# Entry of a ConvFFN's down projection: eight low halves by ScalarE and adding DMAs instead of VectorE and GpSimd

## The chip, the core and the metric

The kernel runs on one core of a Trainium2 chip. A core has TensorE (PE, the matmuls), VectorE (DVE), ScalarE (ACT), GpSimd (POOL) and SyncE (SP), each with an instruction queue of its own that is worked through in order, and 16 DMA engines that the queues of SP, ACT and POOL feed. The metric is the device time of one execution in microseconds (us), lower is better.

## The reference, cut to what matters

The program is one decoder layer: a gated linear attention and a conformer convolution side by side, merged, and then a gated ConvFFN. What the change touches is the last line of the ConvFFN:

```python
u = rms_norm(h, norm_ffn_g[l])
a, bv = jnp.split(u @ w_up[l], 2, axis=-1)
a = causal_dwconv(a, ffn_dw_w[l], ffn_dw_b[l])
h = h + (jax.nn.silu(a) * bv) @ w_down[l]
...
h = rms_norm(h, final_norm_g)
```

The inner width is 2816 (22 tiles of 128 channels), the model width 1024 (8 tiles), and there are 1024 tokens. All is float32.

## The kernel before

**Three matmuls for one.** Every float32 operand x of a matmul is split in two: hi is x rounded to float32r (ACT copies x with AF.Copy into a float32r tile), lo is x - hi, rounded likewise. `mm3` (L178 to L189) gives each product of a weight tile and an operand tile as three matmuls: hi with hi (L187), the weight's hi with the operand's lo (L188), the weight's lo with the operand's hi (L189). In the tiles' names wr is a raw weight piece, wh and wl its halves; ar is a raw activation pair, oph and opl its halves.

**How lo is made.** In the ordinary way DVE (or POOL) subtracts: `lo = raw - hi` (L162 for weights, L228 for operands). `load_w` with POOL as its engine has another way, which the first 51 weight pieces of the program take: ACT writes hi, and also writes the negated rounded value into lo (scale -1, L173); then a DMA issued by POOL adds the raw weight from HBM onto lo (L175, `accum_op=ALU.add`), so that no engine subtracts.

**The stage around the change.** The up projection ends with unit 21 (`unit_head`, `unit_products`: eight products of 24 matmuls; `unit_tail`: taps, Silu, product with the gate, on DVE and ACT). Each unit's result is written to HBM (act_d). The down projection takes the tokens in two halves of 512 (hf 0 and 1). For a half, `load_act` loads the activations of one pair of channel tiles (ar, 128 x 1024) by a DMA issued on POOL (L898) and splits it; there are ten such pairs and an eleventh that is split from SBUF, from the results of units 20 and 21. The weight of an output tile comes in three pieces (8, 8 and 6 channel tiles wide); output tiles 0 and 1 are worked together, so the pieces come as tile 0 first piece (here w0), tile 1 first piece (w1), tile 0 second piece (w2), then w3, w4, w5. One piece of 8 channel tiles against four pairs is 24 matmuls of 512 columns. w0 and w1 need the pairs 0 to 3, w2 and w3 the pairs 4 to 7, w4 and w5 the pairs 8 to 10.

**What sets the order.** A tile scheduler places the instructions; in this stretch `rate["pinned"]` is on, and every ACT copy that makes a hi half is kept in the program's order. The program calls `load_act` for the pairs in turn, with the loads of w0, w1 and w2 behind the pairs 1, 5 and 9. Within a queue an instruction that waits holds back all that stand behind it, a DMA's issue on POOL too. Raw weights have three buffers, hi and lo three each; the activations, their halves and the residual tiles share 35 slots.

Of the kernel before, what the change touches and what calls it, by code (L numbers as in the profile page):

```python
# [11 lines left out]
F32R = mybir.dt.float32r  # L12
U8 = mybir.dt.uint8
AF = mybir.ActivationFunctionType
ALU = mybir.AluOpType
# [24 lines left out]
HT = 516  # L40
# [24 lines left out]
def build(ctx, tc, xT, w_mix, w_o3, w_up, w_dn, w_au, pvec, masks, outT):  # L65
    nc = tc.nc
    V, S, PO, PE = nc.vector, nc.scalar, nc.gpsimd, nc.tensor
# [20 lines left out]
    def slot(dt=F32, nm="s"):  # L88
        uid[0] += 1
        return slots.tile([P, SLOT], dt, tag="slot", name=f"{nm}_{uid[0]}")  # L90
# [6 lines left out]
    def psum():  # L97
        return bank("prod")[:, :512] if "prod" in banks else bank("mm")
# [37 lines left out]
    def load_alpha(src):  # L136
        with tc.high_priority(offset=10000):
            raw = wraw.tile([P, 1024], F32, tag="raw", name="wr_a")
            hl = wspl.tile([P, 1024], F32R, tag="hi", name="wh_a")
            nc.sync.dma_start(raw, src)  # L140
            S.activation(hl, raw, AF.Copy)
            lo, full = (t.rearrange("p (k n) -> p k n", n=P)[:, :, 96:112] for t in (hl, raw))
            V.tensor_tensor(lo, full, lo.bitcast(F32), op=ALU.subtract)
        return hl, None

    def pin(ins):
        if rate["pinned"]:
            tc.keep_in_program_order(ins)

    def load_raw(src):  # L150
        uid[0] += 1
        raw = wraw.tile([P, 1024], F32, tag="raw", name=f"wr_{uid[0]}")[:, : src.shape[-1]]
        nc.sync.dma_start(raw, src)
        return raw

    def split_w(raw, eng=None):
        uid[0] += 1
        n = raw.shape[-1]
        hi = wspl.tile([P, 1024], F32R, tag="hi", name=f"wh_{uid[0]}")[:, :n]
        lo = wspl.tile([P, 1024], F32R, tag="lo", name=f"wl_{uid[0]}")[:, :n]  # L160
        pin(S.activation(hi, raw, AF.Copy))  # L161
        (eng or V).tensor_tensor(lo, raw, hi.bitcast(F32), op=ALU.subtract)  # L162
        return hi, lo

    def load_w(src, eng=None, ahead=4000):
        with tc.high_priority(offset=ahead):
            raw = load_raw(src)
            if eng is not PO:
                return split_w(raw, eng)
            uid[0] += 1  # L170
            hi = wspl.tile([P, 1024], F32R, tag="hi", name=f"wh_{uid[0]}")
            lo = wspl.tile([P, 1024], F32R, tag="lo", name=f"wl_{uid[0]}")
            pin(S.activation(lo, raw, AF.Copy, scale=-1.0))  # L173
            pin(S.activation(hi, raw, AF.Copy))
            nc.gpsimd.dma_start(lo, src, accum_op=ALU.add)  # L175
            return hi, lo

    def mm3(out, whi, wlo, pairs, cols, first=True, last=True):  # L178
        n = len(pairs)
        c0, c1 = cols  # L180
        if wlo is None:
            for k, (wk, (hi, lo)) in enumerate(pairs):
                PE.matmul(out, whi[:, wk], hi[:, c0:c1], start=k == 0, stop=False)
                PE.matmul(out, whi[:, wk], lo[:, c0:c1], start=False, stop=k == n - 1)
            return
        for k, (wk, (hi, lo)) in enumerate(pairs):
            PE.matmul(out, whi[:, wk], hi[:, c0:c1], start=first and k == 0, stop=False)  # L187
            PE.matmul(out, whi[:, wk], lo[:, c0:c1], start=False, stop=False)  # L188
            PE.matmul(out, wlo[:, wk], hi[:, c0:c1], start=False, stop=last and k == n - 1)  # L189

    def operand(t, n=2 * HT, eng=None):
        hi, lo = slot(F32R, "oph"), slot(F32R, "opl")
        split(t[:, :n], hi[:, :n], lo[:, :n], eng)
        return hi, lo

    def block(w, act, chunks, off, evac, mid=None):
        whi, wlo = w
        if mid:
            pts = [psum()[:, :n] for _, n in chunks]
            for k in range(KT):  # L200
                for (c0, n), pt in zip(chunks, pts):
                    mm3(pt, whi, wlo, [(slice(k * P, (k + 1) * P), act[k])], (off + c0, off + c0 + n), k == 0, k == KT - 1)
            rate["pinned"] = True
            mid()
            for (c0, n), pt in zip(chunks, pts):
                pin(evac(pt, c0, n))
            rate["pinned"] = False
            return
        pairs = [(slice(k * P, (k + 1) * P), act[k]) for k in range(KT)]
        for c0, n in chunks:  # L210
            pt = psum()
            mm3(pt[:, :n], whi, wlo, pairs, (off + c0, off + c0 + n))
            evac(pt[:, :n], c0, n)
            tick()
# [11 lines left out]
    def split(src, hi, lo, eng=None):  # L226
        pin(S.activation(hi, src, AF.Copy))
        (eng or V).tensor_tensor(lo, src, hi.bitcast(F32), op=ALU.subtract)  # L228
# [11 lines left out]
        return [tmp512()[:, :n] for i in range(2)] + [None]  # L240

    conv_q, gla_q, ln_q = deque(), deque(), deque()
    rate = {"conv": 0.0, "gla": 0.0, "ln": 0.0, "conv_due": 0.0, "gla_due": 0.0, "ln_due": 0.0, "ahead": 10000, "pinned": False}

    def step(q):
        while q:
# [4 lines left out]
    def tick():  # L251
        for name, q in (("gla", gla_q), ("conv", conv_q), ("ln", ln_q)):
            rate[name + "_due"] = min(rate[name + "_due"] + rate[name], 64.0) if q else 0.0
            while rate[name + "_due"] >= 1.0 and q:
                step(q)
                rate[name + "_due"] -= 1.0
# [34 lines left out]
    order = [NB_A]  # L291
# [8 lines left out]
    w_alpha = seq[0]  # L300
    seq += [w_o3[i] for i in range(16)]
    seq += [w_o3[16 + i] for _ in range(2) for i in range(8)]
    wq = deque()
    wpos = [0]

    def prefetch(n):
        while wpos[0] < len(seq) and len(wq) < n:
            src = seq[wpos[0]]
            wq.append(load_alpha(src) if src is w_alpha else load_w(src, PO if wpos[0] < 51 else V, rate["ahead"]))
            wpos[0] += 1  # L310

    def next_w(ahead=1):
        prefetch(ahead + 1)
        return wq.popleft()
# [65 lines left out]
    def c_pair(i):  # L380
        sg = slot(nm="sg")
        c = slot(nm="c")
        PO.memset(c[:, 0:META], 0.0)
        block(next_w(), u, CHUNKS_L, 0,
              lambda pt, c0, n: S.activation(sg[:, c0 : c0 + n], pt, AF.Sigmoid))
        block(next_w(), u, CHUNKS_L, 0,
              lambda pt, c0, n: V.tensor_tensor(c[:, META + c0 : META + c0 + n], pt, sg[:, c0 : c0 + n], op=ALU.mult))
        conv_q.append(conv(i, c))
# [200 lines left out]
    def r_block(i):  # L589
        og = ogs.pop(i)  # L590
        sr = slot(nm="sr")

        def ev(pt, c0, n):
            sl = slice(c0, c0 + n)
            S.activation(sr[:, sl], pt, AF.Silu)
            PO.tensor_tensor(og[:, sl], og[:, sl], sr[:, sl], op=ALU.mult)

        block(next_w(), u, CHUNKS_Q, T0, ev)
        nc.sync.dma_start(og_d[i], og[:, :LQ])
# [295 lines left out]
    def load_act(hf, j):  # L895
        raw = slot(nm="ar")
        src = act_d[j].rearrange("p (e t) -> p e t", t=SEQ)[:, :, hf * 512 : (hf + 1) * 512]
        nc.gpsimd.dma_start(raw[:, :1024].rearrange("p (e t) -> p e t", t=512), src)  # L898
        return operand(raw, 1024, PO if hf == 0 and j in (8, 9) else V)

    on_pool = (1, 4)
    pieces = [(0, 8), (8, 16), (16, FT)]
# [1 line left out]
    seq[:] = [w_dn[n][:, a * P : b * P] for _ in range(2) for ns in groups for a, b in pieces for n in ns]  # L904
    wpos[0] = len(order)
    seq[:0] = [None] * len(order)

    def finish(hf, c0, cn, h2, pt):
        rs = tmp512()[:, :cn]
        rsqrt_from(pt, rs, cn, RMS_EPS, chunk_tmps(cn))  # L910
        yield 1
        for m in range(KT):
            h = h2[m // 2][:, (m % 2) * 512 + c0 : (m % 2) * 512 + c0 + cn]
            if m in on_pool:
                PO.tensor_tensor(h, h, rs, op=ALU.mult)
            else:
                V.scalar_tensor_tensor(h, h, pcol("fin_g", m), rs, op0=ALU.mult, op1=ALU.mult)
            if m % 2:
                t0 = hf * 512 + c0
                src = h2[m // 2][:, :1024].rearrange("p (e t) -> p e t", t=512)[:, :, c0 : c0 + cn]  # L920
                (nc.sync if m % 4 == 1 else nc.scalar).dma_start(
                    outT[m - 1 : m + 1, :, t0 : t0 + cn].rearrange("e p t -> p e t"), src)
            yield 1
# [3 lines left out]
    for j in range(FT // 2):  # L927
        if j == FT // 2 - 1:
            hi, lo = slot(F32R, "oph"), slot(F32R, "opl")
# [11 lines left out]
    for hf in range(2):  # L941
        if hf:
            acts = [load_act(hf, j) for j in range(FT // 2)]
# [102 lines left out]
```

## Time and profile before

| what | value |
|---|---|
| time, median of 3 runs | 1846.56 us (1845.87 to 1848.41) |
| profiled execution, its own time | 1847.21 us |
| its span, first to last instruction | 1845.4 us |
| PE busy | 1776.2 us (96%) |
| DVE busy | 1156.4 us (63%) |
| ACT busy | 705.6 us (38%) |
| POOL busy | 444.8 us (24%) |
| mean granted TensorE clock | 0.983 |

A time in the rows is counted from the span's first instruction. The matmuls of the down projection begin 1570.88 us into the span. PE's busy time is modelled, and matmuls overlap in it; what PE loses is better read from the starts of its matmuls. In a waits view a line names who waited and for whom, and an idle time in brackets belongs to the instruction behind it. The granted clock is 1.00 at the upper of TensorE's two levels (2.4 GHz) and 0.50 at the lower (1.2 GHz).

### The profile page before, as it was taken

The page shows a single profiled execution, that of the slowest core. Times are in us where ns is not written, and L with a number is a line of the kernel's source. Part 1 is how long each engine was busy: PE and PEld are TensorE (multiplying, and loading weights), DVE is VectorE, ACT ScalarE, POOL GpSimd, SP SyncE. Part 2 cuts the span into 40 slices and gives each one's busy share as a digit, 9 for nine tenths or more (in the row PEclk, how much of TensorE's full clock was granted, in tenths as well). Part 3 has the DMA queues.
Part 4 walks back from the last instruction along what each step waited for, and adds up shares of the span by engine and source line. Part 5 has one row for each costly group of instructions (what it writes and reads, how often), then busy time and mean ns, then how long its engine had stood idle before and what let it go on. Part 6 is the DMA issues. An engine that isn't in the chain of part 4 may idle for free.

```text
span 1845.4 us, 28931 instructions
## 1 busy us (share of the span) xinstructions
PE 1776.2 (96%) x12210; PEld 1692.7 (92%) x12210; DVE 1156.4 (63%) x1350; ACT 705.6 (38%) x1050; POOL 444.8 (24%) x333
## 2 busy tenths in 40 slices
PE   4999999999999999999999997999999999899997
PEld 3999999999999999999999997999999999677886
DVE  5239976968878860733455369877667666733523
ACT  5325436426435743691222333222222223423321
POOL 2103223313413412200000256333333334200000
PEclk7999999999999999999999998999999999999999
DMA  6343335324334544453133441222221224634532
GB/s 211 79 92 87 65 80 125 70 71 114 69 80 103 121 124 120 153 192 137 35 137 129 164 132 35 100 73 77 86 79 69 87 86 151 207 116 154 158 119 66
DMA packets 63442, 200.93 MB, mean 109 GB/s; under 512 B 6864, under 2 KB 14160, under 8 KB 63312
## 3 DMA queue, kind: packets, MB, share of 16 engines
q1 hardware_dynamic: 51168, 159.03, 26.4%
q0 software_dynamic: 10368, 37.75, 10.2%
q10 hardware_dynamic: 1776, 2.30, 0.4%
q8 instruction: 96, 1.57, 0.4%
q14 instruction: 34, 0.28, 0.0%
HBM read 162.31 MB, written 36.74 MB: 108 GB/s over the span
## 4 chain that ended last, share of the span: by engine, by line
PE 80%; DVE 13%; DMA 2%; issue 2%; ACT 2%; POOL 1%; SPq 0%; DVEq 0%; ACTq 0%; POOLq 0%
PE mm L187 13%; PE mm L188 13%; PE mm L189 13%; PE prod L187 12%; PE prod L189 12%; PE prod L188 12%; DVE y L370 5%; DVE opl L228 1%; DVE wl L162 1%; PE g L476 1%; DVE E L445 1%; DMA x<-in_xT 1%; PE g L544 1%; PE g L537 1%; PE g L545 1%
## 5 line engine op out<-in xcount | busy, mean ns | idle before, releaser
L187 PE MATMUL mm<-uh,wh 128*128 128x342 f32 (+4 forms) x1344 | 445.7, 332 | 0.0
L188 PE MATMUL mm<-ul,wh 128*128 128x342 f32 (+4 forms) x1344 | 435.0, 324 | 0.0
L189 PE MATMUL mm<-uh,wl 128*128 128x342 f32 (+4 forms) x1344 | 433.0, 322 | 0.0
L188 PE MATMUL prod<-opl,wh 128*128 128x258 f32 x1232 | 349.7, 284 | 12.1 <-DVE opl L228 11.8
L187 PE MATMUL prod<-oph,wh 128*128 128x258 f32 x1232 | 350.1, 284 | 4.8 <-DVE t L832 4.8
L189 PE MATMUL prod<-oph,wl 128*128 128x258 f32 x1232 | 350.4, 284 | 0.0
L370 DVE SCALAR_TENSOR_TENSOR y<-c,pv,y 128x1026 f32<-128x1026 f32 x240 | 342.3, 1426 | 5.4
L161 ACT ACTIVATE wh<-wr 128x1024 fp32r<-128x1024 f32 (+2 forms) x152 | 147.7, 974 | 382.5 <-PE prod L188 175.2
L162 DVE TENSOR_TENSOR wl<-wr,wh 128x1024 fp32r<-128x1024 f32 (+2 forms) x134 | 159.0, 1189 | 175.6 <-ACT wh L161 174.3
L187 PEld LDWEIGHTS mm<-uh,wh 128*128 128x128 f32 x1344 | 255.7, 190 | 5.4 <-issue 3.7
L188 PEld LDWEIGHTS mm<-ul,wh 128*128 128x128 f32 x1344 | 255.5, 190 | 1.7 <-issue 0.6
L189 PEld LDWEIGHTS mm<-uh,wl 128*128 128x128 f32 x1344 | 255.6, 190 | 0.7 <-issue 0.6
L188 PEld LDWEIGHTS prod<-opl,wh 128*128 128x128 f32 x1232 | 234.4, 190 | 13.3 <-DVE opl L228 12.7
L187 PEld LDWEIGHTS prod<-oph,wh 128*128 128x128 f32 x1232 | 234.4, 190 | 5.8 <-issue 3.2
L189 PEld LDWEIGHTS prod<-oph,wl 128*128 128x128 f32 x1232 | 233.9, 190 | 0.0
L189 PE MATMUL mm<-oph,wl 128*128 128x512 f32 (+1 forms) x374 | 143.6, 384 | 3.2 <-DVE wl L162 3.2
L187 PE MATMUL mm<-oph,wh 128*128 128x512 f32 (+1 forms) x374 | 143.9, 385 | 2.1 <-ACT wh L161 1.3
L188 PE MATMUL mm<-opl,wh 128*128 128x512 f32 (+1 forms) x374 | 144.6, 387 | 0.6 <-DVE opl L228 0.6
L187 PE MATMUL prod<-sh,wh 128*128 128x342 f32 (+2 forms) x448 | 133.8, 299 | 0.5 <-ACT gate L656 0.5
L175 POOL DMA_DIRECT2D wl<-in_w_mix x50 | 44.0, 880 | 372.2 <-ACT wl L173 318.3
L189 PE MATMUL prod<-sh,wl 128*128 128x342 f32 (+2 forms) x448 | 133.4, 298 | 0.0
L188 PE MATMUL prod<-sl,wh 128*128 128x342 f32 (+2 forms) x448 | 133.4, 298 | 0.0
(239 smaller groups left out, 2852.4 us busy)
## 6 DMA issues: line engine op xcount, KB each, us to landing
wr<-in_w_mix SPq DMA_DIRECT2D x56, 512.0 KB, 3.9
wl<-in_w_mix POOLq DMA_DIRECT2D x50, 512.0 KB, 8.1
wr<-in_w_up SPq DMA_DIRECT2D x48, 512.0 KB, 3.3
wr<-in_w_o SPq DMA_DIRECT2D x32, 512.0 KB, 3.5
wr<-in_w_dn SPq DMA_DIRECT2D x32, 512.0 KB, 3.6
act_d<-fy SPq DMA_DIRECT2D x21, 512.0 KB, 2.6
ar<-act_d POOLq DMA_DIRECT2D x21, 512.0 KB, 6.6
wr<-in_w_dn SPq DMA_DIRECT2D x16, 384.0 KB, 3.2
```

What stands on the lines that cost most here:

```text
L161: pin(S.activation(hi, raw, AF.Copy))
L162: (eng or V).tensor_tensor(lo, raw, hi.bitcast(F32), op=ALU.subtract)
L175: nc.gpsimd.dma_start(lo, src, accum_op=ALU.add)
L187: PE.matmul(out, whi[:, wk], hi[:, c0:c1], start=first and k == 0, stop=False)
L188: PE.matmul(out, whi[:, wk], lo[:, c0:c1], start=False, stop=False)
L189: PE.matmul(out, wlo[:, wk], hi[:, c0:c1], start=False, stop=last and k == n - 1)
L228: (eng or V).tensor_tensor(lo, src, hi.bitcast(F32), op=ALU.subtract)
L370: V.scalar_tensor_tensor(y[:, :LQ], c[:, j : j + LQ], pcol("dw_w", i * CONV_K + j), y[:, :LQ], op0=ALU.mult, op1=ALU.add)
L445: V.tensor_tensor(Ev[:, :, 0:s], Ev[:, :, 0:s], kv[:, :, 0:s], op=ALU.mult)
L476: PE.matmul(pt[:, c * half : (c + 1) * half].rearrange("p (b t) -> p b t", t=s), lt[:, sl], right(rt[:, sl], s), start=True, stop=True)
L537: PE.matmul(kv_ps[:, :DVH], kdT[:, c * CH : (c + 1) * CH], vc(c), start=True, stop=True)
L544: PE.matmul(op[:, :DVH], qd[:, c * CH : (c + 1) * CH], sts[c], start=True, stop=False)
```

## The change

For the first token half, the pairs 0 to 4 no longer have their low half subtracted by DVE: ACT writes the high half and then the negated rounded value into the low half, and POOL issues a DMA that adds the raw pair, from SBUF, onto the low half. The weight pieces w0, w1 and w2 take the way of the program's first 51 pieces: two ACT writes and an adding DMA from HBM. Pairs 8 and 9, which POOL split before, are split by DVE. All else is as it was; line numbers behind the new function are 7 or 10 higher.

```diff
+    def operand_by_dma(t, n=2 * HT):
+        hi, lo = slot(F32R, "oph"), slot(F32R, "opl")
+        pin(S.activation(hi[:, :n], t[:, :n], AF.Copy))
+        pin(S.activation(lo[:, :n], t[:, :n], AF.Copy, scale=-1.0))
+        nc.gpsimd.dma_start(lo[:, :n], t[:, :n], accum_op=ALU.add)
+        return hi, lo
+
...
-            wq.append(load_alpha(src) if src is w_alpha else load_w(src, PO if wpos[0] < 51 else V, rate["ahead"]))
+            wq.append(load_alpha(src) if src is w_alpha else load_w(src, PO if wpos[0] < rate["by_dma"] else V, rate["ahead"]))
...
         nc.gpsimd.dma_start(raw[:, :1024].rearrange("p (e t) -> p e t", t=512), src)
-        return operand(raw, 1024, PO if hf == 0 and j in (8, 9) else V)
+        if hf == 0 and j < 5:
+            return operand_by_dma(raw, 1024)
+        return operand(raw, 1024)
...
+    rate["by_dma"] = len(order) + 3
```

POOL's queue at the entry of the down projection, before. The rows are the loads of the pairs 0 to 9 (act_d_10144 to act_d_10153) and the two subtractions of the pairs 8 and 9:

```order
L898 DMA ar_15077<-act_d_10144 128x2x512
L898 DMA ar_15083<-act_d_10145 128x2x512
L898 DMA ar_15095<-act_d_10146 128x2x512
L898 DMA ar_15101<-act_d_10147 128x2x512
L898 DMA ar_15107<-act_d_10148 128x2x512
L898 DMA ar_15113<-act_d_10149 128x2x512
L898 DMA ar_15125<-act_d_10150 128x2x512
L898 DMA ar_15131<-act_d_10151 128x2x512
L898 DMA ar_15137<-act_d_10152 128x2x512
L228 TENSOR_TENSOR opl_15140<-ar_15137,oph_15139 128x1024
L898 DMA ar_15143<-act_d_10153 128x2x512
```

The same place in POOL's queue now, from pair 2 (act_d_10146) to pair 7 (act_d_10151). L905 is the load of a pair, L200 the adding DMA of a pair, L175 the adding DMA of a weight piece (here w0, then w1):

```order
L905 DMA ar_15098<-act_d_10146 128x2x512
L200 DMA opl_15087<-ar_15084 128x1024
L175 DMA wl_15094<-in_w_dn 128x1024
L905 DMA ar_15105<-act_d_10147 128x2x512
L200 DMA opl_15101<-ar_15098 128x1024
L905 DMA ar_15112<-act_d_10148 128x2x512
L200 DMA opl_15108<-ar_15105 128x1024
L905 DMA ar_15119<-act_d_10149 128x2x512
L200 DMA opl_15115<-ar_15112 128x1024
L905 DMA ar_15132<-act_d_10150 128x2x512
L175 DMA wl_15128<-in_w_dn 128x1024
L905 DMA ar_15138<-act_d_10151 128x2x512
```

Before, nine loads stood one behind the other; now every load from pair 2 on stands behind an adding DMA, which itself waits for ACT. The loads of the pairs 8 and 9 and the adding DMA of w2 (wl_15159) follow, in this order.

ACT's queue at the same place, before, from w0 (wh_15091) to w2 (wh_15151):

```order
L161 ACTIVATE wh_15091<-wr_15089 128x1024
L227 ACTIVATE oph_15097<-ar_15095 128x1024
L227 ACTIVATE oph_15103<-ar_15101 128x1024
L227 ACTIVATE oph_15109<-ar_15107 128x1024
L227 ACTIVATE oph_15115<-ar_15113 128x1024
L161 ACTIVATE wh_15121<-wr_15119 128x1024
L227 ACTIVATE oph_15127<-ar_15125 128x1024
L227 ACTIVATE oph_15133<-ar_15131 128x1024
L227 ACTIVATE oph_15139<-ar_15137 128x1024
L227 ACTIVATE oph_15145<-ar_15143 128x1024
L161 ACTIVATE wh_15151<-wr_15149 128x1024
```

And now, from pair 3 (ar_15105) to w2 (wl_15159), where L173 and L199 are the negated writes:

```order
L198 ACTIVATE oph_15107<-ar_15105 128x1024
L199 ACTIVATE opl_15108<-ar_15105 128x1024
L198 ACTIVATE oph_15114<-ar_15112 128x1024
L199 ACTIVATE opl_15115<-ar_15112 128x1024
L234 ACTIVATE oph_15121<-ar_15119 128x1024
L173 ACTIVATE wl_15128<-wr_15125 128x1024
L174 ACTIVATE wh_15127<-wr_15125 128x1024
L234 ACTIVATE oph_15134<-ar_15132 128x1024
L234 ACTIVATE oph_15140<-ar_15138 128x1024
L234 ACTIVATE oph_15146<-ar_15144 128x1024
L234 ACTIVATE oph_15152<-ar_15150 128x1024
L173 ACTIVATE wl_15159<-wr_15156 128x1024
```

The pairs and pieces keep their turn; eight negated writes stand between them, and those of w1 and w2 stand behind the high halves of the pairs 5 and 9. PE's matmuls keep their order; only what they wait for differs: the first L188 and L189 on a pair or piece now wait for the adding DMA's landing.

## Rows read from the trace of the kernel before

**Rows 1.** Waits of PE, 1566 to 1600 us: total us, times, longest us.

```profile
PE mm L189 <- DVE wl L162: 3.2, 2, 1.8
PE mm L187 <- ACT wh L161: 1.3, 1, 1.3
...
PE mm L188 <- DVE opl L228: 0.6, 1, 0.6
```

**Rows 2.** Windows, PE alone: length, busy (instructions), granted clock, DMA share, GB/s.

```profile
1572.00:1574.00 2.00, 0.41 (x1) 0.87 0.01 4
...
1578.00:1580.00 2.00, 2.00 (x6) 0.50 0.36 113
```

**Rows 3.** Timeline of PE: start, duration, line, operation [idle before, releaser].

```profile
1571.92 0.49 PE L188 MATMUL mm<-opl,wh 128*128 128x512 f32 x1 [0.57 <-DVE opl L228]
1574.19 0.80 PE L189 MATMUL mm<-oph,wl 128*128 128x512 f32 x1 [1.78 <-DVE wl L162]
...
1580.33 0.40 PE L188 MATMUL mm<-opl,wh 128*128 128x512 f32 x1
...
1582.64 0.39 PE L189 MATMUL mm<-oph,wl 128*128 128x512 f32 x1
...
1589.72 0.50 PE L189 MATMUL mm<-oph,wl 128*128 128x512 f32 x1 [1.42 <-DVE wl L162]
1590.06 0.39 PE L187 MATMUL mm<-oph,wh 128*128 128x512 f32 x1
...
1594.65 0.39 PE L189 MATMUL mm<-oph,wl 128*128 128x512 f32 x1
...
1597.61 0.45 PE L189 MATMUL mm<-oph,wl 128*128 128x512 f32 x1
```

**Rows 4.** Timeline of DVE, same stretch.

```profile
1574.05 6.81 DVE L228 TENSOR_TENSOR opl<-ar,oph 128x1024 fp32r<-128x1024 f32 x4
...
1586.41 0.80 DVE L850 TENSOR_SCALAR fy<-fa,pv 128x1024 f32<-128x1024 f32 x1
```

**Rows 5.** Tile ar, DVE's subtraction: duration in ns min/median/max, first and last start.

```profile
L228 DVE TENSOR_TENSOR opl<-ar,oph x19: 1211/1221/3430, 1570.6 to 1720.3; 128x1024 fp32r<-128x1024 f32 x19
```

**Rows 6.** Timeline of ACT, same stretch.

```profile
1563.08 1.06 ACT L161 ACTIVATE wh<-wr 128x1024 fp32r<-128x1024 f32 x1 [2.46 <-PE prod L188]
1564.04 1.99 ACT L227 ACTIVATE oph<-ar 128x1024 fp32r<-128x1024 f32 x2
...
1595.19 2.53 ACT L161 ACTIVATE wh<-wr 128x1024 fp32r<-128x1024 f32 x3
```

**Rows 7.** Line L175, adding DMAs of weights: issue in ns, POOL's wait, landing.

```profile
L175 POOL DMA_DIRECT2D wl<-in_w_mix x50: 855/878/1062, 12.7 to 718.9; - x50
...
  ACT wl L173: 318.3, 44
...
DMA to landing us min/median/max: 6.1/8.1/10.9
```

**Rows 8.** Timeline of ACT, one negated write.

```profile
155.07 1.04 ACT L173 ACTIVATE wl<-wr 128x1024 fp32r<-128x1024 f32 x1
```

**Rows 9.** Timeline of POOL, the adding DMA behind that write.

```profile
156.41 0.86 POOL L175 DMA_DIRECT2D wl<-in_w_mix  x1 [11.86 <-ACT wl L173]
```

**Rows 10.** Line L898, loads of pairs: issue in ns, then issue to landing.

```profile
L898 POOL DMA_DIRECT2D ar<-act_d x21: 704/716/791, 1552.1 to 1702.6; - x21
...
DMA to landing us min/median/max: 4.2/6.6/11.3
```

**Rows 11.** Timeline of POOL: the first three loads.

```profile
1552.12 2.25 POOL L898 DMA_DIRECT2D ar<-act_d  x3
```

**Rows 12.** DMA queues, 651 to 668 us, one adding DMA: packets, MB, share.

```profile
q0 software_dynamic: 144, 0.52, 17.6%
```

**Rows 13.** DMA queues, 1550 to 1600 us: some twelve plain transfers.

```profile
q0 software_dynamic: 1707, 6.24, 35.9%
```

**Rows 14.** Line L153, plain loads of weight pieces issued by SP: landing.

```profile
DMA to landing us min/median/max: 3.0/3.6/10.4
```

More of the change, by code (lines that the diff above doesn't have):

```diff
@@ L242, in build @@
     conv_q, gla_q, ln_q = deque(), deque(), deque()
-    rate = {"conv": 0.0, "gla": 0.0, "ln": 0.0, "conv_due": 0.0, "gla_due": 0.0, "ln_due": 0.0, "ahead": 10000, "pinned": False}
+    rate = {"conv": 0.0, "gla": 0.0, "ln": 0.0, "conv_due": 0.0, "gla_due": 0.0, "ln_due": 0.0, "ahead": 10000, "pinned": False, "by_dma": 51}
     def step(q):
```

## Prediction

> **What bounds the kernel now.** I read the page first: PE is busy for 96% of the span, so only a stretch in which PE stands still or runs slowly can give time back. Then the waits of PE in the stretch that the change touches: two waits for a weight's low half (3.2 us together), one for a weight's high half (1.3 us), one for an operand's low half (0.6 us) [rows 1]. Then the granted clock there: it is falling between 1572 and 1574 us (0.87), and between 1578 and 1580 at the lower level, 0.50 [rows 2]. The timeline of PE says what that costs: from 1574.19 to 1580.33 stand 14 matmul steps in 6.14 us, while 20 steps from 1590.06 to 1594.65 take 0.23 us each; 14 such steps are 3.2 us, so the slow stretch costs 2.9 us [rows 3]. The entry loses some 8 us in all, and the queue to blame is DVE's: it subtracts back to back (four in 6.81 us), 1.22 us for one [rows 4, 5].
>
> Three places on PE matter below. The third matmul of w0 (its first L189) starts at 1574.19; that of w1 at 1582.64; that of w2 at 1589.72, after a wait of 1.42 us [rows 3]. From the last of them, 26 steps on, the third matmul of w3 starts at 1597.61. That is 7.89 us for 26 steps, which without a stall take 5.98: 1.9 us more are lost there, most of it the wait for the high half of w3 [rows 1, 3].
>
> **What leaves.** Eight subtractions leave DVE's queue here and two come to it from POOL; the eight are 8 x 1.22 = 9.8 us of DVE [rows 5]. DVE is then no longer what PE waits for in w0, w1 and w2. What is late next is what the low halves now need: the adding DMAs, and ahead of them POOL's queue.
>
> **What is added, and what one link costs.** ACT gains eight negated writes, 0.95 us each when two stand back to back (1.99 us for two) [rows 6]. POOL issues eight adding DMAs at 0.88 us [rows 7]. From the end of a negated write to the start of its DMA's issue go 0.29 us (155.07 + 1.04 against 156.41) [rows 8, 9]. From the start of that issue to the landing, 50 adding DMAs of the same size in this program took 6.1 us at least, 8.1 in the median, 10.9 at most [rows 7]; PE never waited for those, as they were issued far ahead. That POOL waits in its queue for ACT's write is seen there too: 318 us of idle time before 44 of them [rows 7]. The load of a pair takes 0.72 us to issue and lands after 4.2, 6.6 or 11.3 us (least, median, most) [rows 10]. An addition whose source is SBUF is not in the trace; its landing is bounded by the load's least, 4.2, and the weight addition's most, 10.9, and I take the weight addition as nearest, since it too reads its target and writes it back.
>
> **The chain.** Before, the first three loads were issued at once at 1552.12 [rows 11]. Now the load of pair 2 stands behind the addition of pair 0, that of pair 3 behind those of pair 1 and of w0, and so on. Followed from the place that does not move:
>
> - ACT's negated write of w0 takes the place that the high half of w0 had, 1563.08; its buffer is read by PE until one matmul later, so 1563.2 [rows 6]. Done 1564.2, issue of its DMA from 1564.5 to 1565.4. The load of pair 3 starts its issue at 1565.4, at the earliest.
> - Landing, then both halves of pair 3 on ACT (1.99), the way to POOL (0.29), the issue of that addition (0.88): then the load of pair 5 is issued.
> - Landing, then the high half of pair 5 and the negated write of w1 (1.99), 0.29, the addition of w1 (0.88), the loads of the pairs 7 and 8 (1.44): then the load of pair 9 is issued.
> - Landing, then the high half of pair 9 and the negated write of w2 (1.99), 0.29: the addition of w2 is issued, and its landing frees the third matmul of w2.
>
> The fixed links are 1.99 + 0.29 + 0.88 + 1.99 + 0.29 + 0.88 + 1.44 + 1.99 + 0.29 = 10.0 us, so that matmul starts at 1575.4 plus three landings of a load plus one of an addition. With medians: 1575.4 + 3 x 6.6 + 8.1 = 1603.3, against 1589.72 before: 13.6 us later. At the least of every row: 1575.4 + 12.6 + 6.1 = 1594.1, 4.4 later. At the most: 1575.4 + 33.9 + 10.9 = 1620.2, 30.5 later. I take the medians. The load alone in an empty queue would be quicker, but each of the three stands right behind an addition in POOL's queue, and one addition held the DMA engines for 17.6% of 17 us = 3.0 us [rows 12], twice a plain transfer (35.9% of 50 us for some twelve, 1.5 us each [rows 13]): 4.2 + 3.0 = 7.2 is the load's landing by that way, and near its median.
>
> On the way there PE waits too, but each wait is shorter than the last. The addition of w0, issued at 1564.5, lands at 1572.6, so w0's third matmul comes 1.6 us earlier than before. The addition of w1 is issued at 1565.4 + 6.6 + 3.2 + 6.6 + 2.3 = 1584.1 and lands at 1592.2, 9.6 us later than w1's third matmul before. After it 22 steps (5.1 us, or 8.0 at the lower clock) end at 1597.3 to 1600.2, before 1603.3: the last wait swallows the others.
>
> **Behind the last wait.** While it waits for w2, PE has only two matmuls to do in 3 us or more. Before, the clock fell after two idle stretches of 0.57 and 1.78 us around one matmul [rows 2, 3], so I let it fall again and add the 2.9 us. The 1.9 us lost before at w3 go. They stay gone only if w3 is ready: the tail of unit 21 stands on DVE behind the pairs 5 to 9, and starts after pair 9 is split, some 3.4 us after that pair lands at 1593. From its start to w3's high half went 1595.19 - 1586.41 = 8.8 us [rows 4, 6]: 1605.2, one or two more with ACT's added writes, against 1603.3 + 6.0 + 2.9 = 1612. Hidden by 5 us, and beyond it PE stays busy as before.
>
> **The sum.** +13.6 - 1.9 + 2.9 = +14.6 us. The profiled execution took 1847.21 us (its span 1845.4 and 1.8 around it), 0.65 above the median of the three runs, so 1861.8 for it and 1861 for a median. A difference of 0.2% (3.7 us) is about what a measurement of this kernel can tell from no change.
>
> **A page of the skill against the rows.** The 50 additions landed after 6.1 to 10.9 us, the loads of pairs after 4.2 to 11.3 [rows 7, 10]. The Trainium skill, DMA: Bandwidth & Descriptors, section on the anatomy of one DMA by the SWDGE (gpsimd) path, fits one DMA as 2.0 us plus its bytes over 436 GB/s: an estimate of 3.2 us for 512 KB. The trace does not agree for any transfer that POOL issued; by the fit the chain would end at 1588 and the sum would be near the first rival's.
>
> **Rivals.**
>
> - *Short landings* (faster). Each transfer of the chain finds the DMA engines free and lands as soon as SP's plain weight loads do, after 3.0 us at the least and 3.6 in the median [rows 14]. The point that decides: three loads and one addition together must land within 1589.72 + 1.9 - 1575.4 = 16.2 us, 4.0 each, to leave the end where it was. At 3.0 each, w2's third matmul starts at 1587.4, 2.3 us earlier, the 1.9 us of w3 go and the clock need not fall: -4.2 us, 1842; at 3.6 each -1.8 us, 1845. For it: the loads are spread out, so the engines are emptier than before. Against it: the least of POOL's rows sums to 3 x 4.2 + 6.1 = 18.7 [rows 7, 10], and every load of the chain has an addition ahead of it.
> - *Every landing near the least that POOL's rows show*. Chain +4.4, less 1.9, and 0 to 2.9 for the clock: +2.5 to +5.4, 1849 to 1852. For it: fewer loads in the engines at one time. Against it: the 3.0 us that an addition holds them [rows 12].
> - *Landings pile up*, as where single loads took 11.3 us: +30.5 - 1.9 + 2.9 = +31.5, 1878. Against it: the new order itself spaces the issues.
>
> **How the numbers follow.** Medians 0.78, near the least 0.13, pile-up 0.04, short landings 0.05. The predicted time is the medians', 1861. The range, 1851 to 1870, begins inside the near-least case and ends where the three loads take 9.6 us each, 3 above the median and still below the most seen. Below it lie short landings and half of near-least (0.11), above it pile-up and some of the medians' own spread (0.07). Of near-least, 0.04 falls within 3.7 us of no change and the rest above, and of short landings 0.01: slower 0.78 + 0.04 + 0.09 = 0.91, same 0.05, faster 0.04.
>
> **What would show it.** In the profile after: POOL's loads of the pairs 2 to 9 spread from 1559 to beyond 1580 us instead of nine by 1566; PE's waits at w1 and w2 named by a DMA of wl, the longest between 5 and 10 us; the matmuls of w2 starting after 1600; the lower clock more than once; no wait for a subtraction in w0 to w2. It is wrong if additions from SBUF or loads behind them land within 4 us, if POOL's loads are not held back, or if w0's third matmul is the last long wait.

## The result, and the profile after

The changed kernel took 1867.21 us in the median (1865.35 to 1870.56, 4 runs), the kernel before 1847.49 us (1845.87 to 1853.78, 4 runs): ratio 1.0104, 95% interval 1.0087 to 1.0122, so 16 to 23 us slower. The profiled execution took 1867.04 us (its span 1865.3 us), 19.8 us more than that of the kernel before (1847.21).

The loss lies between two matmuls. From w0's first to w4's first went 1602.04 - 1570.88 = 31.2 us before; after, 1622.68 - 1571.76 = 50.9 us, 19.8 more. The entry itself came 0.88 us later than in before's profile; where a start is compared with before below, this 0.88 is taken off.

The waits of the changed kernel from 1566 to 1640 us (who waited, for whom: total us, times, longest us):

```profile
POOL wl L175 <- ACT wl L173: 16.8, 3, 10.4
...
PE mm L189 <- DMA wl<-in_w_dn: 13.3, 3, 5.0
POOL opl L200 <- ACT opl L199: 13.1, 3, 7.1
ACT oph L234 <- DMA ar<-act_d: 11.3, 5, 5.6
ACT oph L198 <- DMA ar<-act_d: 10.9, 3, 6.6
...
PE mm L187 <- ACT wh L174: 3.5, 1, 3.5
...
PE mm L188 <- DMA opl<-ar: 1.8, 1, 1.8
```

Where PE waited for DVE's subtractions before [rows 1], it now waits for adding DMAs: three times for a weight's low half and once for an operand's. The rows also show the ring behind it: POOL waits for ACT, ACT waits for a load, and the load is a DMA that POOL issues. PE's own timeline, the rows with a wait:

```profile
1571.76 0.47 PE L187 MATMUL mm<-oph,wh 128*128 128x512 f32 x1 [0.88 <-DVE fb L853]
1575.99 0.80 PE L189 MATMUL mm<-oph,wl 128*128 128x512 f32 x1 [3.53 <-DMA wl<-in_w_dn]
1584.40 0.63 PE L188 MATMUL mm<-opl,wh 128*128 128x512 f32 x1 [1.83 <-DMA opl<-ar]
1590.25 0.80 PE L187 MATMUL mm<-oph,wh 128*128 128x512 f32 x1 [3.51 <-ACT wh L174]
1596.22 0.80 PE L189 MATMUL mm<-oph,wl 128*128 128x512 f32 x1 [4.75 <-DMA wl<-in_w_dn]
1609.51 0.79 PE L189 MATMUL mm<-oph,wl 128*128 128x512 f32 x1 [5.00 <-DMA wl<-in_w_dn]
...
1618.31 0.39 PE L189 MATMUL mm<-oph,wl 128*128 128x512 f32 x1
```

The second, fifth and sixth rows are the third matmuls of w0, w1 and w2; the last is w3's first L189, which the prediction calls its third matmul (it is the fifth, as a second L187 and a second L188 stand ahead of it). Before they stood at 1574.19, 1582.64, 1589.72 and 1597.61 [rows 3]. From w0's first to w2's third went 18.8 us before and 37.8 us now; from there to w3's third 7.89 us before and 8.80 now. That the loss is in the chain of POOL's queue is read on POOL:

```profile
1565.44 0.88 POOL L175 DMA_DIRECT2D wl<-in_w_dn  x1 [1.70 <-ACT wl L173]
1566.01 0.92 POOL L905 DMA_DIRECT2D ar<-act_d  x1
...
1579.58 0.87 POOL L200 DMA_DIRECT2D opl<-ar  x1 [7.09 <-ACT opl L199]
1580.70 0.74 POOL L905 DMA_DIRECT2D ar<-act_d  x1 [0.25 <-issue]
...
1589.55 0.86 POOL L175 DMA_DIRECT2D wl<-in_w_dn  x1 [4.73 <-ACT wl L173]
1590.12 2.20 POOL L905 DMA_DIRECT2D ar<-act_d  x3
1602.73 0.90 POOL L175 DMA_DIRECT2D wl<-in_w_dn  x1 [10.41 <-ACT wl L173]
```

The L905 rows are the loads of pair 3, of pair 5, and of the pairs 7 to 9; the L175 rows are the additions of w0, w1 and w2. Before, the first three loads went out in 2.25 us [rows 11], the next six by 1566 us, and between these nine stood no instruction that waits for ACT; only pair 9's load stood behind one, POOL's subtraction of pair 8. ACT, which starts on a pair when its load has landed, closes the chain:

```profile
1577.28 1.06 ACT L198 ACTIVATE oph<-ar 128x1024 fp32r<-128x1024 f32 x1 [6.57 <-DMA ar<-act_d]
...
1587.25 1.06 ACT L234 ACTIVATE oph<-ar 128x1024 fp32r<-128x1024 f32 x1 [4.21 <-DMA ar<-act_d]
...
1600.42 1.06 ACT L234 ACTIVATE oph<-ar 128x1024 fp32r<-128x1024 f32 x1 [0.31 <-DMA ar<-act_d]
```

These are the pairs 3, 5 and 9. From the start of a load's issue to its ACT row: 1577.28 - 1566.01 = 11.3 us, 1587.25 - 1580.70 = 6.5 us, and for the third of the three loads, issued near 1591.6, 8.8 us. The addition of w2 was issued at 1602.73, and PE went on at 1609.51: 6.8 us. Adding DMAs of an operand, whose landing no trace had shown:

```profile
L200 POOL DMA_DIRECT2D opl<-ar x5: 867/867/906, 1560.8 to 1583.3; - x5
...
DMA to landing us min/median/max: 4.8/6.3/9.5
```

And PE's windows (length, busy, granted clock, DMA share, GB/s):

```profile
1576.00:1580.00 4.00, 4.00 (x10) 0.50 0.79 224
...
1592.00:1596.00 4.00, 0.00 (x0) 0.50 0.96 257
...
1608.00:1612.00 4.00, 2.49 (x6) 0.56 1.00 343
1612.00:1616.00 4.00, 4.00 (x13) 0.58 1.05 354
```

The clock is at its lower level, 0.50, behind each long wait, no longer in one place only [rows 2].

### The profile page after: what moved, and what is told of

Same layout as the page of the kernel before. It is cut to its first block, busy times and chain, and to the rows that moved or that the text cites. A ratio compares the mean times of both kernels' runs of the same rounds, so it can differ in the third digit from the quotient of the medians.

```text
span 1865.3 us, 28943 instructions
## 1 busy us (share of the span) xinstructions
PE 1780.5 (95%) x12210; PEld 1695.5 (91%) x12210; DVE 1147.8 (62%) x1344; ACT 713.5 (38%) x1058; POOL 446.8 (24%) x339
## 4 chain that ended last, share of the span: by engine, by line
PE 82%; DVE 10%; DMA 2%; issue 2%; ACT 1%; POOL 1%; SPq 0%; DVEq 0%; ACTq 0%; POOLq 0%
PE mm L187 14%; PE mm L188 14%; PE mm L189 13%; PE prod L187 12%; PE prod L189 12%; PE prod L188 12%; DVE y L377 4%; PE g L483 1%; DMA ar<-act_d 1%; PE g L552 1%; PE g L551 1%; PE g L544 1%; DVE un L756 1%; DMA x<-in_xT 1%; DVE E L452 1%
## 5 line engine op out<-in xcount | busy, mean ns | idle before, releaser
L187 PE MATMUL mm<-uh,wh 128*128 128x342 f32 (+4 forms) x1344 | 444.7, 331 | 0.0
L188 PE MATMUL mm<-ul,wh 128*128 128x342 f32 (+4 forms) x1344 | 433.6, 323 | 0.0
L189 PE MATMUL mm<-uh,wl 128*128 128x342 f32 (+4 forms) x1344 | 431.7, 321 | 0.0
L188 PE MATMUL prod<-opl,wh 128*128 128x258 f32 x1232 | 349.7, 284 | 11.7 <-DVE opl L235 11.4
L187 PE MATMUL prod<-oph,wh 128*128 128x258 f32 x1232 | 350.2, 285 | 4.8 <-DVE t L839 4.8
L189 PE MATMUL prod<-oph,wl 128*128 128x258 f32 x1232 | 350.4, 284 | 0.0
L187 PEld LDWEIGHTS mm<-uh,wh 128*128 128x128 f32 x1344 | 254.7, 189 | 5.2 <-issue 3.4
L188 PEld LDWEIGHTS mm<-ul,wh 128*128 128x128 f32 x1344 | 254.5, 189 | 1.5 <-issue 0.3
L189 PEld LDWEIGHTS mm<-uh,wl 128*128 128x128 f32 x1344 | 254.4, 189 | 0.3
L188 PEld LDWEIGHTS prod<-opl,wh 128*128 128x128 f32 x1232 | 234.5, 190 | 12.9 <-DVE opl L235 12.3
L187 PEld LDWEIGHTS prod<-oph,wh 128*128 128x128 f32 x1232 | 234.4, 190 | 5.8 <-issue 4.2
L189 PEld LDWEIGHTS prod<-oph,wl 128*128 128x128 f32 x1232 | 233.9, 190 | 0.0
L189 PE MATMUL mm<-oph,wl 128*128 128x512 f32 (+1 forms) x374 | 146.3, 392 | 13.3 <-DMA wl<-in_w_dn 13.3
L187 PE MATMUL mm<-oph,wh 128*128 128x512 f32 (+1 forms) x374 | 146.1, 391 | 4.4 <-ACT wh L174 3.5
L188 PE MATMUL mm<-opl,wh 128*128 128x512 f32 (+1 forms) x374 | 147.1, 393 | 1.8 <-DMA opl<-ar 1.8
L187 PE MATMUL prod<-sh,wh 128*128 128x342 f32 (+2 forms) x448 | 133.8, 299 | 0.5 <-ACT gate L663 0.5
L189 PE MATMUL prod<-sh,wl 128*128 128x342 f32 (+2 forms) x448 | 133.5, 298 | 0.0
L188 PE MATMUL prod<-sl,wh 128*128 128x342 f32 (+2 forms) x448 | 133.4, 298 | 0.0
L175 POOL DMA_DIRECT2D wl<-in_w_mix x50 | 44.0, 881 | 368.6 <-ACT wl L173 314.6
```

## The experiments

Theory A: what costs is the order of POOL's queue, where a load stands behind an addition that waits for ACT, which waits for an earlier load. Rival B: the additions themselves, each of which holds the DMA engines for 3.0 us [rows 12]. The table has the medians, the ratios to the kernel before with their 95% intervals, and the time from w0's first matmul to w2's third in the profile.

| run | median us | ratio | w0 first to w2 third, us |
|---|---|---|---|
| before | 1846 to 1847 | 1 | 18.8 |
| the change | 1867.21 | 1.0104 (1.0087 to 1.0122) | 37.8 |
| op_only | 1855.76 | 1.0047 (1.0032 to 1.0062) | 27.9 |
| w_only | 1866.57 | 1.0107 (1.0092 to 1.0122) | 37.1 |
| w_only_dve | 1853.95 | 1.0037 (1.0023 to 1.0051) | 27.3 |
| loads_ahead | 1854.01 | 1.0040 (1.0025 to 1.0055) | 22.8 |
| plain_copies | 1856.36 | 1.0049 (1.0034 to 1.0064) | 30.5 |
| loads_ahead_plain | 1844.88 | 0.9987 (0.9978 to 0.9996) | 20.2 |
| w0_behind_pair0 | 1846.36 | 0.9991 (0.9982 to 1.0000) | 18.8 |
| split_ahead | 1843.71 | 0.9986 (0.9977 to 0.9995) | 11.6 |
| split_ahead_w3 | 1844.40 | 0.9986 (0.9976 to 0.9995) | 11.6 |
| split_ahead_w3b | 1840.72 | 0.9968 (0.9957 to 0.9979) | 11.6 |

### op_only: the operands' additions alone

```diff
-    rate["by_dma"] = len(order) + 3
```

> Only the five operand pairs by ACT and adding DMAs; the weight pieces w0 to w2 are split by DVE as before. Theory A (POOL's order: loads stand behind additions that stand behind ACT, and their landings follow one another): the chain to w2 loses the link of w0, which waits for a buffer until 1564, and the last landing of an addition; the loads of the pairs 6 to 9 still stand behind the addition of pair 4. Third matmul of w2 some 25 us after the first matmul of w0 (before 18.8, with the whole change 37.8), time +6 us, 2 to 9. Rival B (the additions hold the DMA engines, 3 us each, whatever the order): five of eight additions, five eighths of the 19.7 us, +12.

It cost 6 to 11 us (ratio 1.0032 to 1.0062; 8.9 between the medians): from the upper half of A's 2 to 9 to a little above it, short of B's +12. The chain is shorter by the links of w0, w1 and w2, and PE's longest wait is now for an operand:

```profile
1582.42 0.80 PE L188 MATMUL mm<-opl,wh 128*128 128x512 f32 x1 [4.61 <-DMA opl<-ar]
...
1599.42 0.80 PE L189 MATMUL mm<-oph,wl 128*128 128x512 f32 x1 [1.41 <-DVE wl L162]
```

### w_only and w_only_dve: the weights' additions alone, with and without POOL's two subtractions

In both, all operands are subtracted; in w_only the pairs 8 and 9 by POOL as before, in w_only_dve by DVE.

```diff
-        if hf == 0 and j < 5:
-            return operand_by_dma(raw, 1024)
-        return operand(raw, 1024)
+        return operand(raw, 1024, PO if hf == 0 and j in (8, 9) else V)   # w_only
+        return operand(raw, 1024)                                         # w_only_dve
```

> Only the three weight pieces by ACT and adding DMAs; operands split by DVE, the pairs 8 and 9 by POOL as before. Theory A: the addition of w1 waits on POOL for the high half of pair 5 and holds the loads of the pairs 7 and 8; POOL's subtraction of pair 8 then holds the load of pair 9, and its subtraction of pair 9 holds the addition of w2. Third matmul of w2 some 35 us after the first of w0, time +14 to +18 us, nearly as slow as the whole change with three of its eight additions. Rival B: three eighths, +7.

> As the run with the three weight pieces alone, but the pairs 8 and 9 are subtracted by DVE, as in the change. Theory A: POOL's two subtractions leave the chain, so the load of pair 9 goes out behind that of pair 8 and the addition of w2 behind ACT alone: third matmul of w2 some 27 us after the first of w0, time +8 to +11, some 6 us less than with the subtractions on POOL although DVE has more to do. Rival B: the same three additions, so the same time as with the subtractions on POOL, +7.

The additions are the same three, yet the one costs 17 to 23 us and the other 4 to 9. POOL in w_only:

```profile
1581.33 1.73 POOL L905 DMA_DIRECT2D ar<-act_d  x2
1591.28 2.82 POOL L235 TENSOR_TENSOR opl<-ar,oph 128x1024 fp32r<-128x1024 f32 x1 [8.22 <-ACT oph L234]
1594.06 0.72 POOL L905 DMA_DIRECT2D ar<-act_d  x1
1599.44 2.35 POOL L235 TENSOR_TENSOR opl<-ar,oph 128x1024 fp32r<-128x1024 f32 x1 [4.65 <-ACT oph L234]
1601.73 0.92 POOL L175 DMA_DIRECT2D wl<-in_w_dn  x1
```

And in w_only_dve:

```profile
1579.13 2.44 POOL L905 DMA_DIRECT2D ar<-act_d  x3
1591.86 0.90 POOL L175 DMA_DIRECT2D wl<-in_w_dn  x1 [10.29 <-ACT wl L173]
```

In w_only the addition of w2 stands behind two subtractions, each waiting for a pair, and pair 9's load stands between the two: w2's issue comes at 1601.73 instead of 1591.86. Its w2 third is 9.8 us later, counted from w0's first. Taken alone, w_only_dve lies at B's +7 and below A's +8 to +11. But B had both runs at the same time, and so it falls: the same additions cost 13 us more by their place in a queue. It follows too that the move of the pairs 8 and 9 to DVE, a part of the change that I had costed on DVE alone, spares the changed kernel another stop in POOL's queue. (These two were the only subtractions of the first half's loaded pairs that POOL did; the eight low halves of the title were all DVE's before.)

### loads_ahead: the whole change, the loads no longer behind additions

```diff
+    for j in range(6):
+        start_act(0, j)
     for j in range(FT // 2):
+        if 0 < j and j + 5 < FT // 2 - 1:
+            start_act(0, j + 5)
```

(`start_act` issues a pair's load; `load_act` then only splits it.)

> The whole change, but POOL issues the loads of the pairs 0 to 6 ahead of the first addition and each later load three to five pairs ahead; the same additions, the same bytes. Theory A: what is chain goes, and what is left is the additions' own time one behind another in POOL's DMA queue (8 of 3 us behind seven loads): third matmul of w2 25 to 31 us after the first of w0, time +6 to +13. Rival B: nothing that it counts has changed, +17 to +21.

The order alone gives back some 12 us of the 19.7, and w2's third matmul comes sooner than A had it (22.8 us against 25 to 31). What is left, 5 to 10 us, is of another kind. POOL, PE's windows and the landing of the operands' additions:

```profile
1550.40 5.14 POOL L907 DMA_DIRECT2D ar<-act_d  x7
```

```profile
1574.00:1582.00 8.00, 2.55 (x6) 0.50 1.05 289
```

```profile
DMA to landing us min/median/max: 14.0/16.3/17.9
```

Seven loads go out in one row, the DMA engines are fully busy (share 1.05), and an operand's addition takes 14.0 us or more where it took 4.8 to 9.5. With the order mended, B is what is left.

### plain_copies and loads_ahead_plain: the additions as copies of the same bytes

```diff
-        nc.gpsimd.dma_start(lo[:, :n], t[:, :n], accum_op=ALU.add)
+        nc.gpsimd.dma_start(lo[:, :n], t[:, :n])
```

and likewise for w0, w1 and w2.

> The whole change, with each of the eight adding DMAs replaced by a DMA that copies the same bytes over the low half instead of adding them (the eight low halves are then the raw values; the order of every queue is kept). Theory A (the chain of loads held behind additions in POOL's in-order queue): the order still holds, only the transfers ahead of each load take 1.5 us of the DMA engines less, so the first load of the chain (two additions ahead of it) comes 3 us sooner and each later link 1.5 us: w2's third matmul some 30 us after w0's first (whole change: 37.8; before: 18.8), time +11 to +14 us. Rival B (the additions' time in the DMA engines is the cost): w2's third matmul at 24 us or less, time +6 us or less.

> loads_ahead (the pairs' loads issued six pairs early, ahead of the additions that held them), with the eight additions replaced by plain copies of the same bytes (the eight low halves are then the raw values). In loads_ahead +7.2 us was left, w2's third matmul came 22.8 us after w0's first, and the DMA engines were busy all through. Theory A': what was left there is the engines' time: an addition holds them 3.0 us, a copy 1.5. Eight of them give back 12 us of engine time, the landings of the low halves shorten, w2's third matmul comes 18 to 20 us after w0's first, and the time is -2 to +3 us. Rival: what was left is the way ACT - POOL - landing itself, whatever the engines do: w2's third at 22 us or more, time +6 to +8.

In plain_copies w2's third matmul comes 30.5 us after w0's first, as A had it (30), and the time is 6 to 12 us above before (9.5 between the medians, A's range began at 11; B's +6 or less and its 24 us fall). PE:

```profile
1587.31 0.80 PE L192 MATMUL mm<-oph,wl 128*128 128x512 f32 x1 [3.40 <-DMA wl<-in_w_dn]
...
1599.28 0.50 PE L192 MATMUL mm<-oph,wl 128*128 128x512 f32 x1 [3.56 <-DMA wl<-in_w_dn]
```

The landing of the operands' copies in the same run:

```profile
DMA to landing us min/median/max: 2.9/4.9/6.3
```

The load of pair 3, issued at 1563.01, was on ACT at 1571.15: 8.1 us instead of 11.3. So the additions' own length accounts for 3 us of this link and for 7.3 us of the chain (37.8 - 30.5), and the order for most of the rest, 11.7 us more than before. (With the order mended as well, below, 1.4 us of it stay.) In loads_ahead_plain the operands' copies landed so:

```profile
DMA to landing us min/median/max: 10.5/11.9/12.7
```

Against 16.3 us for the additions, with the engines as full (share 1.11 from 1574 to 1582 us, against 1.05). The time is 1 to 4 us below before, the lower edge of A's -2 to +3, and its rival (+6 to +8) falls. The two causes together are thus all of the loss: take both away and the change is no slower than before. They can't be added up one by one: the order mended alone gave back some 12 us, the additions shortened alone some 10, together more than the 19.7 that were lost.

### w0_behind_pair0, split_ahead, split_ahead_w3, split_ahead_w3b: the entry without additions

If DVE's order is what the entry lost its 8 us to, moving subtractions should win it. The first moves w0 alone:

```diff
-        if j in (1, 5, 9):
+        if j in (0, 5, 9):
```

> The kernel before, with the load and split of w0 asked for behind pair 0 instead of behind pair 1, so that on DVE and ACT w0's halves come ahead of pair 1's. If the wait for w0's low half (1.78 us before) and the clock's fall behind it hang together, w0's third matmul comes about 1.1 us earlier, pair 1's low half as much later but hidden, and the time is -1 to -4 us (-4 if the clock stays at its upper level). Rival: the wait only moves to pair 1's low half (1.2 us), the clock falls as before: 0 within 0.5 us.

Measured 0 to 3 us less: not told apart from its rival by the time, and each was half right, as the clock stayed up and the waits remained. PE's waits, 1566 to 1640 us:

```profile
PE mm L189 <- DVE wl L162: 3.8, 3, 1.9
PE mm L188 <- DVE opl L228: 2.2, 2, 1.7
PE mm L187 <- ACT wh L161: 2.1, 2, 1.2
```

Without the 0.9 us ahead of the very first matmul, the waits are more in sum than before (7.2 against 5.1 us [rows 1]); the granted clock, in this one profile, stayed at 1.00 in every window of 4 us from 1564 to 1612. What the clock gave was lost to the waits.

split_ahead makes room: DVE stands idle ahead of the last unit's last evacuations, and the low halves of pair 0, pair 1 and w0 are subtracted there.

```diff
-    def unit_products(ws, head):
+    def unit_products(ws, head, early=None):
...
+            if early:
+                rate["pinned"] = True
+                early()
-            V.tensor_tensor(t2, product(w21, 0, T[2]), p1, op=ALU.add)
+            pin(V.tensor_tensor(t2, product(w21, 0, T[2]), p1, op=ALU.add))
...
+        def early():
+            rate["pin_lo"] = True
+            for j in range(2):
+                acts.append(load_act(0, j))
+            rate["ahead"] = 0
+            prefetch(1)
+            rate["pin_lo"] = False
...
-        if j in (1, 5, 9):
+        if j in (5, 7):
```

(`pin_lo` keeps these subtractions in the program's order.)

> The kernel before, with the low halves of pair 0, pair 1 and w0 subtracted by DVE ahead of the last unit's last evacuations, in a stretch where DVE stands idle for some 9 us, and w1 and w2 asked for behind the pairs 5 and 7. If DVE's queue at the entry is what costs the 8 us there, the matmuls of w0 start without the two waits, the clock stays at its upper level, w2's third matmul comes 15 to 17 us after w0's first (before 18.8), and the time is -4 to -8 us. Rival: the evacuations that now stand behind the splits hold PE in the last unit, or the splits wait for their loads and hold DVE: the loss moves ahead, time 0 to +4 us.

The stalls of w0, w1 and w2 went altogether: w2's third stands 11.6 us behind w0's first, 50 steps of 0.23 us. The time fell by 1 to 4 us only, less than the 4 to 8 expected. PE, and then ACT:

```profile
1591.02 0.80 PE L189 MATMUL mm<-oph,wh 128*128 128x512 f32 x1 [5.19 <-ACT wh L161]
```

```profile
1585.62 1.06 ACT L868 ACTIVATE fy<-fy 128x1024 f32<-128x1024 f32 x1 [3.59 <-DVE fy L866]
...
1589.91 2.52 ACT L161 ACTIVATE wh<-wr 128x1024 fp32r<-128x1024 f32 x3
```

The high half of w3 stands on ACT behind the Silu of unit 21 (L868), which waits for DVE's taps: the gain was given back there. So w3 is asked for earlier, behind pair 9 or behind pair 8:

```diff
-        if j in (5, 7):
+        if j in (5, 7, 9):   # split_ahead_w3
+        if j in (5, 7, 8):   # split_ahead_w3b
```

> split_ahead, with w3 asked for behind pair 9 as well, so that its high half stands on ACT ahead of the last unit's Silu and no longer behind it. In split_ahead PE ran from w0's first matmul to the end of w2 without a stall, then waited 5.2 us for w3's high half, and the clock fell: some 3 us more. Theory: that one wait is what ate the gain. w3's high half is then ready before 1584, the wait goes, the last unit's tail on DVE ends 1.2 us later, and w4's low half comes 1 to 2 us late in its place: -7 to -10 us against the kernel before (some 1837 to 1840). Rival: what DVE subtracts earlier for w3 only pushes the tail, and the wait reappears at w4 with the same size: -3 us, as split_ahead.

> As split_ahead_w3, with w3 asked for behind pair 8 instead of behind pair 9: on ACT its high half needs only w0's matmuls to be done, and on DVE its low half stands ahead of the whole tail of the last unit instead of within it. Theory: the same time as split_ahead_w3 within 1 us (-7 to -10 us), since the tail is 1.2 us later in both. Rival: pair 9's halves on ACT, now one place later, hold w4: 1 to 2 us slower than split_ahead_w3.

In both the wait for w3 is gone, and from w0's first matmul to w4's first go 23.0 and 23.1 us (before 31.2). split_ahead_w3b is 4 to 8 us faster than before, the fastest of all that ran; split_ahead_w3 only 1 to 4 us. Both stay short of the 7 to 10 expected, and neither theory nor rival had split_ahead_w3b ahead of split_ahead_w3. Their intervals just touch; why the two differ, if they do, isn't settled. Both lose some of it further on, at 1605.75 and 1609.57 us, where PE sums the squares of the outputs and DVE has the squares (t) late. PE's wait in split_ahead_w3, and then in split_ahead_w3b:

```profile
PE g L987 <- DVE t L986: 2.6, 1, 2.6
```

```profile
PE g L987 <- DVE t L986: 2.2, 1, 2.2
```

Behind it the clock fell in the one profile (0.70 from 1604 to 1608 us) and not in the other (1.00). One profile of each can't say whether that is the rule. The fall doesn't explain why split_ahead_w3 is slower, either: its eleven runs reach from 1840.7 to 1846.9 us, and the profile with the fall is that of the fastest.

## Why the prediction was right, and which term was mis-sized

The forecast was +14.6 us, 1861; measured +19.7, within the range and with the sign given 0.91. The mechanism is the one forecast, link for link; the size of one term, the landings, was off.

- **The start of the chain** held: ACT's negated write of w0 at 1564.08, the issue of its addition at 1565.44, the load of pair 3 at 1566.01, against 1563.2, 1564.5 and 1565.4 plus the 0.88 of the later entry. This link was forecast to within 0.3 us.
- **The fixed links** were 10.0 us; from pair 3's load to w2's third matmul went 43.5 us, of which 33.4 us were the four landings, so 10.1.
- **The landings** were mis-sized: 3 x 6.6 + 8.1 = 27.9 us taken, 11.3 + 6.5 + 8.8 + 6.8 = 33.4 us measured. The 5.5 us between them are as much as the sum is off (19.7 - 14.6 = 5.1). Most of it is the first, pair 3's load: it took 11.3 where I had the median of all loads, 6.6, and had reasoned that one addition ahead of a load costs 3.0 us, 7.2 in all. Two were ahead, that of pair 1 and that of w0, issued 3.2 and 0.6 us before it, besides the load of pair 2. plain_copies shows the size: with copies in their place the same load takes 8.1 us. The third load, pair 9's, did not stand right behind an addition, as the prediction says of all three, but behind one and two other loads: 8.8 us. The last addition landed 1.3 us sooner than its median, which hid a part of the error.
- **The price of one addition was right, the count was not.** In w_only_dve pair 3's load has one addition ahead of it, that of w0, and POOL had issued nothing for 10 us before. POOL, and then ACT on pair 3:

```profile
1565.09 0.90 POOL L175 DMA_DIRECT2D wl<-in_w_dn  x1 [10.18 <-ACT wl L173]
1565.69 2.88 POOL L905 DMA_DIRECT2D ar<-act_d  x4
```

```profile
1573.51 1.06 ACT L234 ACTIVATE oph<-ar 128x1024 fp32r<-128x1024 f32 x1 [6.83 <-DMA ar<-act_d]
```

That is 1573.51 - 1565.69 = 7.8 us, near the 7.2. In op_only, behind the additions of the pairs 0 and 1 and a load, the same load takes 9.3 us (1563.25 to 1572.51).
- **w0's third matmul** was forecast 1.6 us earlier than before and came 0.9 later: its addition took 10.5 us to land (1565.44 to 1575.99), near the most of the 50 seen [rows 7], most likely for the same reason, the addition of pair 1 ahead of it. It changed nothing, as the last wait swallowed it, which the text had for w1.
- **Behind the last wait** -1.9 and +2.9 made +1.0; measured 8.80 - 7.89 = +0.9. The tail of unit 21 was hidden, as forecast.
- **Waits not named**: 1.8 us for pair 3's addition and 3.5 us for w1's high half, which stands on ACT behind pair 5. Both lie ahead of the last wait and are swallowed by it.
- **The signs listed** came: loads to 1592 us, w2 after 1600 (first matmul at 1603.89), the lower clock in three places, no wait for a subtraction in w0 to w2. The longest wait, 5.0 us, is at the edge of the 5 to 10 given, since PE lost more before it than I had counted.
- **The rivals.** Short landings needed 16.2 us for four; they took 33.4. Near-least (18.7) fell as well. Pile-up came true in one of the four links: pair 3's load took as long as the most that a load had shown.
- **A reading of DVE that was off.** Four subtractions in 6.81 us are 1.70 us each, not 1.22. One of them and a later one took 3.40 and 3.43 us (the most in [rows 5]), and these are the two that ran while POOL subtracted the pairs 8 and 9, from 1574.31 and from 1582.91. No term of the sum hangs on it.
- **The Trainium skill's fit.** The least landing of a plain copy, 2.9 us in plain_copies, is near the 3.2 us that the Trainium skill, DMA: Bandwidth & Descriptors, section on the anatomy of one DMA by the SWDGE path, would give as an estimate for 512 KB. Its median, 4.9, is not, and an addition's 4.8, 6.3 and 9.5 us lie wholly above it. The section gives the fit per DMA; in this chain no load that followed an addition was alone.

What was shown: that the order costs (loads_ahead, w_only against w_only_dve) and that an addition's length costs (plain_copies, loads_ahead_plain). What was only argued: that it is the additions under way alone that lengthen pair 3's load from 7.8 to 9.3 and 11.3 us; no run changes their number and leaves the other loads beside them as they are.

## What to carry to other kernels

A DMA that waits for an engine holds every later DMA of its queue, so before a subtraction is moved into a DMA, look at what stands behind it in that queue and whether it feeds the same engine: here the ring POOL, ACT, load, POOL cost 12 us of 20. Price a landing by what is issued just ahead of it, not by the median of its line. When a stall goes, follow each queue to the next instruction that waits in order: split_ahead lost its gain to one Silu on ACT, and asking for a piece earlier brought back some 3 us of it in one of two tries.

## What the runs showed of the hardware that was not expected

- An operand's adding DMA takes POOL 0.87 us to issue in the changed kernel, a copy of the same shape 0.55 us (plain_copies, 1573.46 to 1574.01), so the queue of additions is slower already where it is issued. One of the three copies of a weight took 0.85 us, though.
- On full DMA engines (loads_ahead and loads_ahead_plain, share 1.05 and 1.11) the landing of an SBUF to SBUF addition stretched to 14.0 to 17.9 us and that of a copy to 10.5 to 12.7, from 4.8 to 9.5 and 2.9 to 6.3.
- The clock did not fall in w0_behind_pair0 through six waits of 0.6 to 1.9 us with matmuls between them, though their sum is larger than that of the kernel before, where it fell behind two waits around one matmul [rows 2, 3]. One profile each.
- In the kernel before, a DVE subtraction of a pair took 1.21 to 1.23 us, but 3.40 and 3.43 us in the two cases that ran beside a subtraction on POOL. In the changed kernel, where POOL subtracts no pair, DVE's five at the entry all took 1.22 to 1.23 us.
